# Reordering the split products of four down stages in an encoder trunk on one Trainium2 core

## The chip, the cores and the metric

The kernel runs on one core of one Trainium2 chip, in one launch. A core has five engines that work side by side, each on its own list of instructions: TensorE (PE in the profile, with PEld for its weight loads), VectorE (DVE), ScalarE (ACT), GpSimd (POOL) and SyncE (SP, which here only issues transfers). Sixteen DMA engines carry the transfers. The metric is the device time of one execution in microseconds; the time of a kernel is the median of its runs.

## The reference

A trunk of two layers over 512 positions of width 1024, in float32. Cut to what matters here:

```python
for i in range(DEPTH):                       # DEPTH = 2, D_MODEL = 1024, D_FF = 2816, SEQ = 512
    h = h + 0.5 * swiglu(rmsnorm(h, norm_ffn1[i]), ffn1_w_gate[i], ffn1_w_up[i], ffn1_w_down[i])
    hn = rmsnorm(h, norm_mix[i])
    h = h + (ab_mixer(hn, ...) if i % 2 == 0 else c_mixer(hn, ...))
    h = h + 0.5 * swiglu(rmsnorm(h, norm_ffn2[i]), ffn2_w_gate[i], ffn2_w_up[i], ffn2_w_down[i])
    gate = jax.nn.sigmoid(rmsnorm(h, norm_ple[i]) @ w_ple_gate[i])
    h = h + gate * (p[i] @ w_ple_proj[i])
return rmsnorm(h, norm_final)

def swiglu(x, w_gate, w_up, w_down):
    return (jax.nn.silu(x @ w_gate) * (x @ w_up)) @ w_down
```

The last product of `swiglu`, by `w_down` (2816 x 1024), is the down stage. There are four of them.

## The kernel before

Every float32 product is made of three matmuls: each operand is split into a rounded high part and the rest, and high x high, high x low and low x high are added up in PSUM. The split of a weight unit is `split` (lines 150 and 151): ScalarE copies the high part (`wh`), VectorE subtracts it from the raw weights to get the low part (`wl`). A raw unit is 128 x 1024 floats, 512 KB, and lies in a tile `wr`.

**Tiles.** Tiles of each kind come from a fixed number of slots: 5 `wr`, 4 each of `wh` and `wl`, 8 `tmp` of 128 x 512, 62 `act` of 128 x 512, and the PSUM banks 3 `mm`, 2 `sc`, 2 `tr` and 1 `ob`. A tile needs a slot before its first write, and waits until the last use of the tile that had the slot.

**Order.** A planner goes over the program once and fixes the order of the instructions on each engine by estimated times and priorities; the engines then execute in that order and wait for each other through semaphores. Within one kind of tile, slots are handed out in the order of the program. `high_priority()` moves instructions up, and `issue_after(x)` keeps the instructions issued inside it behind x on x's own engine.

**A down stage** (`down`, lines 434 to 620) has 22 chunks of 128 rows. The first four (`wide`, `xs`) are multiplied in the plain way by the `left` and `right` halves of the weights. The other 18 are taken as nine pairs (A, B), and w_down as four quarters b11, b12, b21 and b22 of nine chunks, and the block product is done with seven products in place of eight: some with sums of activations (`inner_sums`: x3), some with sums of weight quarters. Quarters come in five units: four of two chunks and one of one chunk. A weight sum is not calculated by an engine: `load` (L474, SP) brings one quarter to a `wr` tile, and `add` (L478, POOL) issues a second transfer that adds another quarter into the same tile, over and over along a chain:

```python
b11 -> r1 += x1,   + b12 -> r3 += x1 (right),    # group 1, r2 += x2 with b21 beside it
b12 + b22 -> rb += x3,  + b11 -> r1 += x3 (right),  + b21 -> rc += x2 (right)   # group 2
```

The order of a stage before is: rx (24 matmuls, the four wide chunks by `right`), copied to `cx`; group 1 in steps s = 0 to 5, where step s has r1 and r2 of unit s and the fifth product r3 of unit s-1; the left wide product into r2; the additions of r2 to the copies of r1 (L538); group 2 in steps s = 0 to 6, where step s has rb of unit s, r1 of unit s-1 and rc of unit s-2, and the left-hand wide product into rc in steps 0 and 1; and the tail: the right wide units once more, then b22 by x4, both into r3, among the transposes and the norm's splits. rc has the banks that r2 had, so its first product waits for L538. `halves` of 512 columns, as the pair stages of the feed-forward do them in tiles named `rb` (L366 to L369), are the only weight loads of 256 KB.

**The other places.** Each norm's sum of squares (`ssq`, L226) is turned into a factor per position by `stat`: eight small matmuls (L233), VectorE (L235), GpSimd's power (L236); `spread` transposes it (L252) and ScalarE copies it to `R` (L260). The property `rcol` makes the statistic on first use, and `R` the copy. In group c (the neighbourhood mixer, `c`, L1141) `self.rcol` stands first, and `project_v` (L694, matmuls L712 to L714) makes the values. The gate stage (`ple`, L1294) multiplies chunks 0 and 1 of the gate with the inner products first, then takes `R` and goes through the eight chunks, with t1 at L1333.

Of the kernel before, what the change touches and what calls it, by code (L numbers as in the profile page):

```python
# [10 lines left out]
F32R = mybir.dt.float32r  # L11
# [4 lines left out]
P = 128  # L16
# [32 lines left out]
class Trunk:  # L49
# [408 lines left out]
    def down(self, w, a, xs, sums, kept):  # L458
# [13 lines left out]
        def load(b, u):  # L472
            raw = self.wr.tile([P, UNIT], F32, tag="wr", name=self.nm("wr"))[:, :len(u) * T]
            nc.sync.dma_start(raw, b[:, u.start * T:u.stop * T])  # L474
            return raw

        def add(raw, b, u):
            nc.gpsimd.dma_start(raw, b[:, u.start * T:u.stop * T], accum_op=ALU.add)  # L478

        def product(out, u, ws, xs, cols, start=False, stop=False):  # L480
            mm = nc.tensor.matmul
            for j, k in enumerate(u):
                wh, wl = (x[:, j * T:(j + 1) * T] for x in ws)
                for i, p in enumerate(out):
                    c = slice(cols.start + i * P, cols.start + (i + 1) * P)
                    xh, xl = (x[:, c] for x in xs[k])
                    mm(p, xh, wh, start=start and k == 0, stop=False, skip_group_check=True)  # L487
                    mm(p, xh, wl, start=False, stop=False, skip_group_check=True)
                    mm(p, xl, wh, start=False, stop=stop and k == u.stop - 1, skip_group_check=True)

        def copied(p):
            out = [self.act() for _ in p]
# [4 lines left out]
        r1, r3 = [self.bank(), self.bank()], [self.sbank(), self.sbank()]  # L497
        r2 = [self.bank(), self.obank()]
        x1, x2, x3, x4 = ([None] * K2 for _ in range(4))
        n, raws = len(units), {}  # L500
        last = lambda u: u.stop == K2

        rx = [self.tbank(), self.tbank()]
        for u in wide:
            for k in u:
                xs[k] = xs[k] or self.split_chunk(a[k], nc.vector)
            product(rx, u, self.parts(load(right, u)), xs, r, True, u.stop == WHOLE)
        cx = copied(rx)

        def summed(s):  # L510
            raws[s] = load(b12, units[s])
            add(raws[s], b22, units[s])

        for s in range(n + 1):
            if s < n:
                u = units[s]
                raw = raws[s] = load(b11, u)
                for k in u:
                    if sums[k] is None:
                        sums[k] = self.inner_sums(A[k], B[k])  # L520
                    x1[k] = self.split_chunk(A[k], nc.vector)
                product(r1, u, self.parts(raw), x1, l, True, last(u))
                add(raw, b12, u)
                raw = load(b21, u)
                for k in u:
                    x2[k] = self.split_chunk(B[k], nc.vector)
                product(r2, u, self.parts(raw), x2, l, True)
            if s:
                u = units[s - 1]
                product(r3, u, self.parts(raws[s - 1]), x1, r, True, last(u))  # L530

        summed(0)
        ws = [self.parts(load(left, u)) for u in wide]
        for u, ww in zip(wide, ws):
            product(r2, u, ww, xs, l, False, u.stop == WHOLE)
        c11, c5 = copied(r1), cx
        for o, p in zip(c11, r2):
            tt(o, p, o, op=ALU.add)  # L538

        rb, rc = [self.tbank(), self.tbank()], [self.bank(), self.obank()]  # L540
        for s in range(n + 2):
            if s + 1 < n:
                summed(s + 1)
            if s < n:
                u = units[s]
                for k in u:
                    x3[k] = self.split_chunk(sums[k], nc.vector)
                    tt(B[k][:, l], B[k][:, l], sums[k][:, r], op=ALU.add)
                product(rb, u, self.parts(raws[s]), x3, l, True, last(u))
                add(raws[s], b11, u)  # L550
            if s < len(wide):
                product(rc, wide[s], ws[s], xs, r, True)
            if s == 1:
                for o, p in zip(c5, r3):
                    tt(o, p, o, op=ALU.add)
            if 0 < s <= n:
                u = units[s - 1]
                product(r1, u, self.parts(raws[s - 1]), x3, r, False, last(u))
                add(raws[s - 1], b21, u)
            if s == n + 1:  # L560
                c2 = copied(r1)
                u3 = [self.act(), self.act()]
                for i in range(2):
                    tt(u3[i], c2[i], rb[i], op=sub)
                for i in range(2):
                    tt(c5[i], c5[i], u3[i], op=sub)
            if s > 1:
                u = units[s - 2]
                product(rc, u, self.parts(raws[s - 2]), x2, r, False, last(u))
                for k in u:  # L570
                    t = self.act(F32R)
                    x4[k] = t[:, l], t[:, r]
                    self.split(B[k][:, l], *x4[k])
        c21 = [self.act(), self.act()]
        for i in range(2):
            tt(c21[i], rc[i], u3[i], op=ALU.add)
# [25 lines left out]
                self.h[m + j] = h  # L602
                self.norm_split(m + j, c)

        for u in wide:
            product(r3, u, self.parts(load(right, u)), xs, l)
        for i, u in enumerate(units):
            product(r3, u, self.parts(load(b22, u)), x4, l, False, last(u))
            if i < 2:
                second_half(M + 2 * i, c22, r)  # L610
            elif i < 4:
                first_half(2 * i - 4)
                first_half(2 * i - 3)
# [84 lines left out]
    def project_v(self, src, view, rcol, parts=True, banks=None):  # L698
# [5 lines left out]
        for q in range(2):  # L704
            u = self.unit(src[:, q * UNIT:(q + 1) * UNIT], lo_eng=self.lo_eng())
            for kk in range(4):
                k = 4 * q + kk
                h, l = (x[:, kk * 256:(kk + 1) * 256] for x in u)
                for b in range(NB):
                    xh, xl = (view(x, b) for x in self.xg[k])  # L710
                    first, last = k == 0 and b % 2 == 0, k == KC - 1 and b % 2 == 1
                    nc.tensor.matmul(ps[b], xh, h, start=first, stop=False, skip_group_check=True)  # L712
                    nc.tensor.matmul(ps[b], xh, l, start=False, stop=False, skip_group_check=True)
                    ins = nc.tensor.matmul(ps[b], xl, h, start=False, stop=last, skip_group_check=True)  # L714
            if q == 0:
                self.half_v = ins
        out = []
        for b in range(NB):
            r = rcol[:, b:b + 1]
# [111 lines left out]
    def ab(self, k_next):  # L831
# [60 lines left out]

        def proj_v(key, i):
            if i < 2:
                f = lambda: v.__setitem__(key, self.project_v(io["v_ab"][i], nat, self.rcol, banks=None if i else [
                    self.sbank(), self.bank()]))
            else:
                f = lambda: v.__setitem__(key, self.residues(
                    self.project_v(io["v_ab"][i], nat, self.rcol, parts=False)))
            return [(key, 2.4, f)]  # L900
# [239 lines left out]

    def c(self, k_next):  # L1141
        nc, io = self.nc, self.io
        self.rcol


        sel = [[self.act(F32R) for _ in range(2)] for _ in range(2)]
# [57 lines left out]

        first = [self.obank(), self.bank()]
        self.mm_units(first, [self.unit(io["qk_c"][i], lo_eng=self.lo_eng()) for i in range(2)])
        fill, steps = [], []
        for n in range(KC):
            fill += [(("q", n), 1, lambda n=n: proj_q(n, None if n else first[0])),
                     (("k", n), 1, lambda n=n: proj_k(n, None if n else first[1]))]  # L1210
            if n % 2 == 0:
                fill.append((("v", n // 2), 2, lambda i=n // 2: vs.__setitem__(
                    i, self.project_v(io["v_c"][i], nat, self.rcol, banks=None if i else [self.sbank(), self.bank()]))))
            need = [("q", n), ("k", n)]
            for hf in range(2):
                steps.append((need, 1, lambda n=n, hf=hf: soft(n, hf)))
                if (n, hf) == (KC - 1, 0):
                    begin = len(steps)
                if n + hf:
                    m, hm = (n, 0) if hf else (n - 1, 1)  # L1220
                    steps.append(([("v", m // 2)], 1, lambda m=m, hm=hm: pv(m, hm)))
# [73 lines left out]
    def ple(self, i, k_next, regroup):  # L1295
# [7 lines left out]
        up, ends, first = None, [], []  # L1303
        for m in range(KC):
            self.fetch(self.kept, m)
            u = first[m][0] if m < len(first) else self.unit(io["plg"][i, m])
            if m % 4 == 0:
                up = self.unit(io["plp"][i, m // 4])
            s = m % 4 * 2 * P
# [1 line left out]
            if m == 0:  # L1311
# [4 lines left out]
                        self.mm_unit(q, tuple(x[:, j * 2 * P:(j + 1) * 2 * P] for x in up), p, True, True)  # L1316

                self.mm_units([f[1] for f in first], [f[0] for f in first], inner)

            half = k_next == N_NORM - 1 and m == KC - 1  # L1320
            for x in (slice(0, T // 2), slice(T // 2, T)) if half else (slice(0, T),):
                cut = lambda parts: [tuple(y[:, x] for y in c) for c in parts]
                if m < len(first):
                    pg, pp = first[m][1:]
                else:
                    pg, pp = self.bank()[:, x], self.sbank()[:, x]
                    self.mm_unit(pg, u, cut(xg), True, True)
                    self.mm_unit(pp, upm, cut(p), True, True)
                if m == 0:
                    R = self.R  # L1330
# [205 lines left out]
```

## Time and profile before

| | |
|---|---|
| median of the runs | 2065.73 us (2065.39 to 2075.05, 3 runs) |
| the profiled execution | 2069.41 us, span 2067.6 us |
| granted TensorE clock, mean over it | 0.994 |
| TensorE busy | 2013.6 us in 12438 matmuls |
| VectorE, ScalarE, GpSimd busy | 1595.9, 1121.0 and 282.9 us |
| the four down stages | about 238 to 359, 880 to 1000, 1289 to 1408 and 1871 to 1992 us |

Busy time is the time in which an engine executed something; the span is from the first to the last instruction. A row "A <- B: total, times, longest" in the list of waits says that the instructions A stood idle until B was done. Timelines have start, duration, engine, line, operation and tiles, and in brackets the idle time before and its releaser. Windows give for each engine (TensorE, weight loads, VectorE, ScalarE, GpSimd) the busy time and the number of instructions in a stretch, then the granted clock, the DMA engines' busy share and GB/s.

### The profile page before, as it was taken

Reading aid. Unit: us, or ns where it says so; the run is one execution under the profiler, and the core shown is the slowest. Engines: PE = TensorE matmul, PEld = TensorE weight load, DVE = VectorE, ACT = ScalarE, POOL = GpSimd, SP = SyncE. Lnnn points to the kernel's source line nnn. Section 1 sums busy time; section 2 is a strip of 40 time slices with the busy share of each in tenths; the row PEclk is TensorE's granted clock in tenths of the full one; section 3 lists DMA queues with packets and bytes.
Section 4 is the critical chain, followed back from the end, with each engine's and each line's share of the span. In section 5 each row is a group of like instructions: output and inputs, shape, how many; then the busy total and the mean of one; then the engine's idle time right before and its main releaser. Section 6 shows DMA issues by size and latency. Waiting matters only on the chain.

```text
span 2067.6 us, 33144 instructions
## 1 busy us (share of the span) xinstructions
PE 2013.6 (97%) x12438; PEld 1786.7 (86%) x12438; DVE 1595.9 (77%) x2743; ACT 1121.0 (54%) x1898; POOL 282.9 (14%) x318
## 2 busy tenths in 40 slices
PE   9999999999999999999999999999999999999898
PEld 6999877879788899977789999778888889998776
DVE  8888866798766888876778888767788678888575
ACT  6455645477645455564544555645666445556452
POOL 0000021342212000012210000112000200001221
PEclk9999999999999999999999999999999999999999
DMA  6666679543425566579644666796333446666881
GB/s 195 179 183 180 166 175 259 168 93 81 98 62 173 128 179 184 161 176 214 229 153 128 184 174 175 183 221 196 108 112 98 160 116 174 179 164 169 187 275 41
DMA packets 126896, 334.90 MB, mean 162 GB/s; under 512 B 23696, under 2 KB 31376, under 8 KB 126736
## 3 DMA queue, kind: packets, MB, share of 16 engines
q1 hardware_dynamic: 98880, 245.71, 35.8%
q0 software_dynamic: 27712, 87.05, 24.1%
q8 instruction: 97, 1.59, 0.3%
q14 instruction: 63, 0.52, 0.1%
q10 hardware_dynamic: 144, 0.04, 0.0%
HBM read 304.42 MB, written 17.27 MB: 156 GB/s over the span
## 4 chain that ended last, share of the span: by engine, by line
PE 79%; DMA 7%; DVE 6%; issue 4%; ACT 3%; POOL 1%; SPq 0%; POOLq 0%; ACTq 0%; DVEq 0%
PE mm L391 6%; PE mm L390 6%; PE mm L392 6%; DMA wr<-in_dn_dram 5%; PE mm L176 5%; PE mm L175 5%; PE mm L177 5%; PE sc L392 3%; PE sc L391 3%; PE sc L390 3%; PE sc L175 2%; PE sc L177 2%; PE sc L176 2%; DVE wl L151 2%; PE ob L392 2%
## 5 line engine op out<-in xcount | busy, mean ns | idle before, releaser
L150 ACT ACTIVATE wh<-wr 128x1024 fp32r<-128x1024 f32 (+2 forms) x499 | 511.5, 1029 | 499.8 <-DMA wr<-in_dn_dram 126.5
L151 DVE TENSOR_TENSOR wl<-wr,wh 128x1024 fp32r<-128x1024 f32 (+2 forms) x499 | 594.2, 1195 | 190.5 <-ACT wh L150 186.2
L392 PE MATMUL mm<-act,wl 128*128 128x256 f32 x1088 | 307.9, 283 | 0.0
L391 PE MATMUL mm<-act,wh 128*128 128x256 f32 x1088 | 307.9, 283 | 0.0
L390 PE MATMUL mm<-act,wh 128*128 128x256 f32 x1088 | 307.9, 283 | 0.0
L175 PE MATMUL mm<-act,wh 128*128 128x512 f32 (+1 forms) x632 | 247.5, 393 | 1.1 <-ACT act L213 0.5
L177 PE MATMUL mm<-act,wl 128*128 128x512 f32 (+1 forms) x632 | 247.4, 391 | 0.5 <-DVE wl L151 0.5
L176 PE MATMUL mm<-act,wh 128*128 128x512 f32 (+1 forms) x632 | 247.1, 392 | 0.6 <-DVE act L214 0.6
L390 PEld LDWEIGHTS mm<-act,wh 128*128 128x128 f32 x1088 | 208.9, 192 | 0.2
L391 PEld LDWEIGHTS mm<-act,wh 128*128 128x128 f32 x1088 | 208.9, 192 | 0.2
L392 PEld LDWEIGHTS mm<-act,wl 128*128 128x128 f32 x1088 | 208.9, 192 | 0.0
L390 PE MATMUL sc<-act,wh 128*128 128x256 f32 x544 | 154.0, 283 | 0.0
L391 PE MATMUL sc<-act,wh 128*128 128x256 f32 x544 | 154.0, 283 | 0.0
L392 PE MATMUL sc<-act,wl 128*128 128x256 f32 x544 | 154.0, 283 | 0.0
L368 POOL DMA_DIRECT2D wr<-in_gu_dram x68 | 59.3, 872 | 678.0 <-DMA wr<-in_gu_dram 240.2
L176 PEld LDWEIGHTS mm<-act,wh 128*128 128x128 f32 x632 | 118.9, 188 | 23.9 <-DVE act L214 2.4
L175 PEld LDWEIGHTS mm<-act,wh 128*128 128x128 f32 x632 | 118.8, 188 | 23.7 <-ACT act L213 1.7
L177 PEld LDWEIGHTS mm<-act,wl 128*128 128x128 f32 x632 | 118.8, 188 | 22.3 <-DVE wl L151 1.3
L478 POOL DMA_DIRECT2D wr<-in_dn_dram x80 | 69.6, 944 | 420.5 <-DVE wl L151 319.6
L487 PE MATMUL mm<-wh,act 128*128 128x512 f32 x248 | 98.2, 396 | 13.8 <-DVE act L538 9.0
L151 DVE TENSOR_TENSOR act<-act,act 128x512 fp32r<-128x512 f32 (+1 forms) x176 | 105.9, 630 | 6.9 <-ACT act L150 6.9
L390 PEld LDWEIGHTS sc<-act,wh 128*128 128x128 f32 x544 | 104.4, 192 | 0.0
(253 smaller groups left out, 4746.1 us busy)
## 6 DMA issues: line engine op xcount, KB each, us to landing
wr<-in_gu_dram SPq DMA_DIRECT2D x176, 512.0 KB, 4.5
wr<-in_dn_dram SPq DMA_DIRECT2D x88, 512.0 KB, 4.3
wr<-in_gu_dram POOLq DMA_DIRECT2D x68, 512.0 KB, 5.5
wr<-in_dn_dram POOLq DMA_DIRECT2D x64, 512.0 KB, 6.3
rb<-in_gu_dram SPq DMA_DIRECT2D x68, 256.0 KB, 2.5
act<-kept SPq DMA_DIRECT2D x56, 256.0 KB, 5.6
wr<-in_qk_ab_dram SPq DMA_DIRECT2D x20, 512.0 KB, 4.0
kept<-act POOLq DMA_DIRECT2D x32, 256.0 KB, 3.0
```

The source lines that it names most:

```text
L150: self.put(self.nc.scalar.activation(hi, src, AF.Copy))
L151: self.put((lo_eng or self.nc.vector).tensor_tensor(lo, src, hi.bitcast(F32), op=ALU.subtract))
L175: mm(out, stat[0], mov[0], start=start, stop=False)
L176: mm(out, stat[0], mov[1], start=False, stop=False)
L177: return mm(out, stat[1], mov[0], start=False, stop=stop)
L368: nc.gpsimd.dma_start(rs, w[:, :UNIT], accum_op=ALU.add)
L390: mm(out, w[0][:, c], xs[k][0][:, x], start=start and k == 0, stop=False, skip_group_check=True)
L391: mm(out, w[0][:, c], xs[k][1][:, x], start=False, stop=False, skip_group_check=True)
L392: mm(out, w[1][:, c], xs[k][0][:, x], start=False, stop=stop and k == half - 1, skip_group_check=True)
L478: nc.gpsimd.dma_start(raw, b[:, u.start * T:u.stop * T], accum_op=ALU.add)
L487: mm(p, xh, wh, start=start and k == 0, stop=False, skip_group_check=True)
```

## The change

Five things are changed, and the matmuls remain the same in number.

1. In group 1 the fifth product r3 of unit s-2, not s-1, follows step s; the last two come behind the left wide product.
2. Group 2 begins with rb of unit 0 ahead of the left wide product; in its loop the order is seventh (rb), sixth (r1), fourth (rc). The wide rc product comes as a whole ahead of the loop, and the second use of the right wide units goes from the tail into steps 2 and 3. The differences u3 are taken one step earlier.
3. Weights that belong to no sum (right, left, b21 and b22) are loaded in halves of 256 KB to `tmp` tiles and split half by half (`halved`); `wr` is left to the chain of sums.
4. In c and ab the statistic of v's factor is issued behind the first half of the first v projection, which in c is traced ahead of the weave; `self.rcol` at the top of c goes.
5. In the gate stage chunk 2's 24 matmuls are issued ahead of the statistic, into a bank of their own.

```diff
+        def halved(b, u):
+            hi = self.wh.tile([P, UNIT], F32R, tag="wh", name=self.nm("wh"))
+            lo = self.wl.tile([P, UNIT], F32R, tag="wl", name=self.nm("wl"))
+            raws = [self.tmp() for _ in u]
+            for raw, k in zip(raws, u):
+                nc.sync.dma_start(raw, b[:, k * T:(k + 1) * T])
+            for j, raw in enumerate(raws):
+                c = slice(j * T, (j + 1) * T)
+                self.split(raw, hi[:, c], lo[:, c])
+            return hi, lo
...
-            product(rx, u, self.parts(load(right, u)), xs, r, True, u.stop == WHOLE)
+            product(rx, u, halved(right, u), xs, r, True, u.stop == WHOLE)
         cx = copied(rx)
+        rb = [self.tbank(), self.tbank()]
...
+        def first(s):
+            u = units[s]
+            raw = raws[s] = load(b11, u)
+            for k in u:
+                if sums[k] is None:
+                    with self.tc.issue_after(marks[s - 2].ins):
                         sums[k] = self.inner_sums(A[k], B[k])
+                x1[k] = self.split_chunk(A[k], nc.vector)
+            marks.append(product(r1, u, self.parts(raw), x1, l, True, last(u)))
+            add(raw, b12, u)
+        def second(s):                    # x2 splits, product(r2, u, halved(b21, u), x2, l, True)
+        def fifth(s):                     # product(r3, u, self.parts(raws[s]), x1, r, True, last(u))
+        def seventh(s):                   # x3 splits, product(rb, ...), add(raws[s], b11, u)
+        def sixth(s):                     # product(r1, ..., x3, r), add(raws[s], b21, u)
+        def fourth(s):                    # product(rc, ..., x2, r), x4 splits
...
+        for s in range(n):
+            first(s)
+            second(s)
+            if s > 1:
+                fifth(s - 2)
+        c11, c5 = copied(r1), cx
         summed(0)
-        ws = [self.parts(load(left, u)) for u in wide]
+        seventh(0)
+        ws = [halved(left, u) for u in wide]
         for u, ww in zip(wide, ws):
             product(r2, u, ww, xs, l, False, u.stop == WHOLE)
-        c11, c5 = copied(r1), cx
+        summed(1)
         for o, p in zip(c11, r2):
             tt(o, p, o, op=ALU.add)
+        fifth(n - 2)
+        fifth(n - 1)
+        rc = [self.bank(), self.obank()]
+        for u, ww in zip(wide, ws):
+            product(rc, u, ww, xs, r, True)
+        for o, p in zip(c5, r3):
+            tt(o, p, o, op=ALU.add)
+        for s in range(1, n + 2):
             if s + 1 < n:
                 summed(s + 1)
             if s < n:
+                seventh(s)
+            if s <= n:
+                sixth(s - 1)
+            if s > 1:
+                fourth(s - 2)
+            if s in (2, 3):
+                u = wide[s - 2]
+                product(r3, u, halved(right, u), xs, l)
+            if s == n:
                 c2 = copied(r1)
...
-        for u in wide:
-            product(r3, u, self.parts(load(right, u)), xs, l)
         for i, u in enumerate(units):
-            product(r3, u, self.parts(load(b22, u)), x4, l, False, last(u))
+            product(r3, u, halved(b22, u), x4, l, False, last(u))
... project_v
             if q == 0:
                 self.half_v = ins
+                if callable(rcol):
+                    with self.tc.issue_after(ins.ins):
+                        rcol = rcol()
... c
-        self.rcol
...
+        vs[0] = self.project_v(io["v_c"][0], nat, lambda: self.rcol, banks=[self.sbank(), self.bank()])
... ple
-            u = first[m][0] if m < len(first) else self.unit(io["plg"][i, m])
+            u = first[m][0] if m < len(first) else next_u if m == 2 else self.unit(io["plg"][i, m])
...
                 self.mm_units([f[1] for f in first], [f[0] for f in first], inner)
+                next_u, ahead = self.unit(io["plg"][i, 2]), self.bank()
+                self.mm_unit(ahead, next_u, xg, True, True)
...
-                    pg, pp = self.bank()[:, x], self.sbank()[:, x]
-                    self.mm_unit(pg, u, cut(xg), True, True)
+                    pg, pp = (ahead if m == 2 else self.bank())[:, x], self.sbank()[:, x]
+                    if m != 2:
+                        self.mm_unit(pg, u, cut(xg), True, True)
```

More of the change, by code (lines that the diff above doesn't have):

```diff
@@ L488, in product @@
                     mm(p, xh, wl, start=False, stop=False, skip_group_check=True)
-                    mm(p, xl, wh, start=False, stop=stop and k == u.stop - 1, skip_group_check=True)
+                    ins = mm(p, xl, wh, start=False, stop=stop and k == u.stop - 1, skip_group_check=True)
+            return ins
         def copied(p):
@@ L499, in down @@
         x1, x2, x3, x4 = ([None] * K2 for _ in range(4))
-        n, raws = len(units), {}
+        n, raws, marks = len(units), {}, []
         last = lambda u: u.stop == K2
@@ L512, in summed @@
             add(raws[s], b22, units[s])
[L514 to L519, printed above, removed]
-                        sums[k] = self.inner_sums(A[k], B[k])
[L521 to L530, printed above, removed]
+        def first(s):
[4 more added lines that the diff above has]
+                    with self.tc.issue_after(marks[s - 2].ins):
+                        sums[k] = self.inner_sums(A[k], B[k])
+                x1[k] = self.split_chunk(A[k], nc.vector)
+            marks.append(product(r1, u, self.parts(raw), x1, l, True, last(u)))
+            add(raw, b12, u)
@@ new lines, in second @@
+        def second(s):
+            u = units[s]
+            for k in u:
+                x2[k] = self.split_chunk(B[k], nc.vector)
+            product(r2, u, halved(b21, u), x2, l, True)
+        def fifth(s):
+            u = units[s]
+            product(r3, u, self.parts(raws[s]), x1, r, True, last(u))
+        def seventh(s):
+            u = units[s]
+            for k in u:
+                x3[k] = self.split_chunk(sums[k], nc.vector)
+                tt(B[k][:, l], B[k][:, l], sums[k][:, r], op=ALU.add)
+            product(rb, u, self.parts(raws[s]), x3, l, True, last(u))
+            add(raws[s], b11, u)
@@ new lines, in sixth @@
+        def sixth(s):
+            u = units[s]
+            product(r1, u, self.parts(raws[s]), x3, r, False, last(u))
+            add(raws[s], b21, u)
+        def fourth(s):
+            u = units[s]
+            product(rc, u, self.parts(raws[s]), x2, r, False, last(u))
+            for k in u:
+                t = self.act(F32R)
+                x4[k] = t[:, l], t[:, r]
+                self.split(B[k][:, l], *x4[k])
+        for s in range(n):
[3 more added lines that the diff above has]
+                fifth(s - 2)
@@ L532, in down @@
+        c11, c5 = copied(r1), cx
         summed(0)
-        ws = [self.parts(load(left, u)) for u in wide]
+        seventh(0)
+        ws = [halved(left, u) for u in wide]
         for u, ww in zip(wide, ws):
             product(r2, u, ww, xs, l, False, u.stop == WHOLE)
-        c11, c5 = copied(r1), cx
+        summed(1)
         for o, p in zip(c11, r2):
             tt(o, p, o, op=ALU.add)
-        rb, rc = [self.tbank(), self.tbank()], [self.bank(), self.obank()]
-        for s in range(n + 2):
+        fifth(n - 2)
@@ L544, in down @@
             if s < n:
[L545 to L560, printed above, removed]
+                seventh(s)
[7 more added lines that the diff above has]
+            if s == n:
                 c2 = copied(r1)
@@ L566, in down @@
                     tt(c5[i], c5[i], u3[i], op=sub)
[L567 to L573, printed above, removed]
         c21 = [self.act(), self.act()]
@@ L894, in proj_v @@
             if i < 2:
-                f = lambda: v.__setitem__(key, self.project_v(io["v_ab"][i], nat, self.rcol, banks=None if i else [
-                    self.sbank(), self.bank()]))
+                f = lambda: v.__setitem__(key, self.project_v(
+                    io["v_ab"][i], nat, self.rcol if i else lambda: self.rcol, banks=None if i else [self.sbank(), self.bank()]))
             else:
@@ L1210, in c @@
                      (("k", n), 1, lambda n=n: proj_k(n, None if n else first[1]))]
-            if n % 2 == 0:
+            if n % 2 == 0 and n:
                 fill.append((("v", n // 2), 2, lambda i=n // 2: vs.__setitem__(
-                    i, self.project_v(io["v_c"][i], nat, self.rcol, banks=None if i else [self.sbank(), self.bank()]))))
+                    i, self.project_v(io["v_c"][i], nat, self.rcol))))
             need = [("q", n), ("k", n)]
```

## The prediction

> **What bounds the kernel now.** I read the page first, then the waits of TensorE, then the timeline and the stage windows around the longest of them. Page, busy time:
>
> ```profile
> PE 2013.6 (97%) x12438; PEld 1786.7 (86%) x12438; DVE 1595.9 (77%) x2743; ACT 1121.0 (54%) x1898; POOL 282.9 (14%) x318
> ```
>
> TensorE is busy for 2013.6 of 2067.6 us, so the change, which leaves the number of matmuls as it is, can only shorten what TensorE waits for, and the time it loses at half clock. Its waits (releaser, then total us, times, longest):
>
> ```profile
> PE mm L487 <- DVE act L538: 9.0, 4, 3.9
> PE sc L488 <- DVE wl L151: 5.1, 6, 2.0
> PE mm L487 <- ACT act L150: 4.8, 4, 1.2
> PE tr L252 <- POOL rcol L236: 4.7, 4, 1.8
> PE tr L233 <- DVE ssq L226: 3.7, 2, 2.9
> PE ob L176 <- POOL act L151: 2.7, 4, 0.7
> PE sc L487 <- ACT wh L150: 2.6, 2, 1.8
> PE mm L488 <- DVE wl L151: 2.0, 6, 0.4
> ```
>
> L487 to L489 are the products of the four down stages. Rows one, two, seven and eight are 9.0 + 5.1 + 2.6 + 2.0 = 18.7 us in 18 waits, all in those stages. Row five is the norm sum ahead of the middle group c, row four mostly the gate products. Rows three and six are not touched.
>
> The longest wait of the third down stage, in the timeline of all engines (start, length, engine, line, idle before):
>
> ```profile
> 1341.54 1.06 ACT L150 ACTIVATE wh<-wr 128x1024 fp32r<-128x1024 f32 x1 [4.26 <-DMA wr<-in_dn_dram]
> ...
> 1342.49 0.39 PE L489 MATMUL tr<-wh,act 128*128 128x512 f32 x1
> ...
> 1342.63 1.23 DVE L151 TENSOR_TENSOR wl<-wr,wh 128x1024 fp32r<-128x1024 f32 x1 [3.06 <-ACT wh L150]
> ...
> 1346.17 0.68 DVE L538 TENSOR_TENSOR act<-ob,act 128x512 f32<-128x512 f32 x1
> 1346.31 0.19 PEld L487 LDWEIGHTS mm<-wh,act 128*128 128x128 f32 x1 [3.86 <-DVE act L538]
> 1346.31 0.50 PE L487 MATMUL mm<-wh,act 128*128 128x512 f32 x1 [3.44 <-DVE act L538]
> ```
>
> The reader is to see a chain that begins at a transfer: a summed weight lands, ScalarE splits it, VectorE stood idle 3.06 us for that split with the two additions of L538 queued behind, and the product rc, which wants the two banks that L538 reads, stands last. The late sum costs twice, at its own product and at the next one.
>
> **What one wait costs.** A run of 24 products in a row gives the cadence, from its first and its last:
>
> ```profile
> 1289.34 0.40 PE L487 MATMUL tr<-wh,act 128*128 128x512 f32 x1
> ...
> 1294.58 0.39 PE L489 MATMUL tr<-wh,act 128*128 128x512 f32 x1
> ```
>
> (1294.58 - 1289.34) / 23 = 0.228 us, so a unit of two chunks (12 matmuls) is 2.7 us and a step of three such units 8.2. From 1342.49 to 1346.31 are 3.82 us, 3.59 more than the cadence, where the row says 3.44; with a first matmul that is also slow to follow on I add 0.25 us to each wait. Then the clock (stretch, its length, five pairs of busy time, granted clock, DMA share, GB/s):
>
> ```profile
> 982.08:985.50 3.42, 3.42 (x10) 2.64 (x9) 1.97 (x2) 0.80 (x1) 0.00 (x0) 0.50 1.02 383
> ...
> 1930.98:1934.39 3.41, 3.41 (x10) 2.67 (x9) 2.50 (x6) 0.00 (x0) 0.00 (x0) 0.50 1.05 204
> 1425.81:1432.64 6.83, 6.45 (x30) 6.16 (x31) 1.58 (x5) 1.04 (x2) 1.03 (x1) 0.50 0.00 0
> ```
>
> These are the first and the last of three such stretches in down stages, and the one in c. At 0.50 half of 3.41 us is lost, 1.7 us. What comes before the first of them is this:
>
> ```profile
> 980.70 0.50 PE L488 MATMUL sc<-wl,act 128*128 128x512 f32 x1 [1.82 <-DVE wl L151]
> ```
>
> A wait of 1.82 us, next to some shorter ones, was followed by half clock. [...]
>
> **The change, part by part.**
>
> Down, gross. 18.7 us of waits, 18 x 0.25 = 4.5 for restarts, 3 x 1.7 = 5.1 of clock: 28.3 us in four stages. What removes them:
>
> (1) Two steps between a sum and its use. The sum is issued by POOL on a tile that has just been split. How long it takes to land:
>
> ```profile
> DMA to landing us min/median/max: 4.4/6.5/11.3
> ```
>
> (the answer for L478). With the full-width splits
>
> ```profile
> L150 ACT ACTIVATE wh<-wr 128x1024 fp32r<-128x1024 f32 x466 | 491.8, 1058 | 445.3 <-DMA wr<-in_dn_dram 85.4 <-PE mm L176 70.4 <-ACT wh L150 52.7
> ```
>
> that chain is 6.5 + 1.06 + about 1.2 on VectorE = 8.8 us at the median and 13.6 at the most. Before, the last fifth product has two units of cover, 5.4 us: it waits. After, at least seventh(0), two wide left units and a second's product lie between, 11 us or more: the median is covered, the maximum nearly. (2) rc now follows fifth(n-2) and fifth(n-1), 4.1 us behind the last read of its banks where it was one unit, 2.7; and L538 no longer queues behind a split that waits for a transfer, since seventh(0) is ahead of it. (3) The right wide units leave the tail for steps 2 and 3, and no longer wait there. (4) `issue_after(marks[s-2].ins)` names a TensorE instruction around three VectorE ones; as an order within an engine it holds nothing back, zero. I keep 2.3 us of small waits: down is -26.
>
> Down, new work. Some 15 units a stage are now loaded and split in halves. Rows of existing halves and wholes, transfer (KB, median us to landing) and split:
>
> ```profile
> wr<-in_gu_dram SPq DMA_DIRECT2D x176, 512.0 KB, 4.5
> ...
> rb<-in_gu_dram SPq DMA_DIRECT2D x68, 256.0 KB, 2.5
> ...
> wr<-in_dn_dram SPq DMA_DIRECT2D x16, 256.0 KB, 4.6
> ```
> ```profile
> L150 ACT ACTIVATE wh<-rb 128x512 fp32r<-128x512 f32 x68 | 42.4, 623 | 0.0
> ```
>
> Two halves on ScalarE are 1.25 us for 1.06, 15 x 0.19 = 3 us a stage; VectorE's part grows alike, and SP has 15 more issues. What hides them is the idle share of each:
>
> ```profile
> 1285.00:1346.00 61.00, 56.28 (x260) 45.36 (x258) 46.88 (x69) 37.60 (x57) 10.47 (x12) 1.00 0.75 182
> 1346.00:1408.00 62.00, 61.69 (x277) 51.06 (x278) 41.27 (x58) 29.96 (x42) 8.11 (x11) 0.97 0.92 239
> ```
>
> VectorE (third pair) is busy 46.9 and 41.3 us, ScalarE 37.6 and 30.0, so zero on average; but the 5.5 us of wide products that covered VectorE in the tail are gone, and I charge 0.25 us a stage, 1 us in all, with bounds 0 and 8 (2 us a stage, the longest wait on a split, row two).
>
> (5) rx starts later. Its four halves now need `tmp` tiles, and slots go out in the order of the program, so theirs come behind those of the last pair of ffn, whose last one is used here:
>
> ```profile
> 1288.32 0.69 DVE L413 TENSOR_TENSOR tmp<-sc,tmp 128x512 f32<-128x512 f32 x1
> ```
>
> rx began at 1289.34 with no wait, as its `wr` tiles were loaded before. If the load goes out only with L413: 1288.32 + 2.5 to land (4.6 by the slower row) + 0.62 + 0.7 of splits = 1292.1 (1294.2), a wait of 2.8 (4.9) us. If SP runs ahead: 0. L413's row does not show whether SP is held by it, so I take the middle of 0 and 2.8, rounded up to 1.5 us: 4 x 1.5 = +6 us, bounds 0 and 4 x (4.9 + 1.7) = 26.
>
> (6) Group c. L233 is put behind 48 of v0's matmuls; only 24 stood ahead of it:
>
> ```profile
> 1422.56 0.28 PE L714 MATMUL mm<-wh,act 128*128 128x256 f32 x1
> 1425.71 1.74 PE L233 MATMUL tr<-ones,ssq 128*128 128x1 f32 x8 [2.87 <-DVE ssq L226]
> ...
> 1428.89 1.12 PE L252 MATMUL tr<-ident,rcol 128*128 128x128 f32 x4 [0.38 <-POOL rcol L236]
> ```
>
> At 0.12 us each (half the width of the others) the other 24 fill 2.9 of the 2.87 + 0.25. The 6.83 us at half clock go with it, half of that, but little more than 3 us, as waiting for L252 is part of it. With 0.38 + 0.25 that is 6.7 at best; if L252 then waits for ScalarE and POOL with nothing left of v0, up to 3 us come back. I take -5.5, bounds -6.7 and -2. In ab the same edit meets no wait of L233 in the list beyond row five: zero.
>
> (7) Gate products (twice). 24 matmuls of chunk 2 now go ahead of the norm sum:
>
> ```profile
> 1017.80 0.95 PE L233 MATMUL tr<-ones,ssq 128*128 128x1 f32 x8
> ```
> ```profile
> 1021.09 0.65 PE L252 MATMUL tr<-ident,rcol 128*128 128x128 f32 x4 [1.76 <-POOL rcol L236]
> ...
> 1027.49 0.39 PE L175 MATMUL mm<-act,wh 128*128 128x512 f32 x1
> ```
> ```profile
> 1022.41 0.69 DVE L1333 TENSOR_TENSOR tmp<-mm,R 128x512 f32<-128x512 f32 x1 [2.27 <-ACT R L260]
> ```
>
> That the planner puts L233 where the program has it, next to the end of the opening products, moves it 24 x 0.228 = 5.5 us later. Then only 6 matmuls (1.4 us) are left to cover the 3.29 us from L233 to L252, and chunk 3 has to wait for the bank that L1333 frees, some 1.9 us behind L252 (1022.41 + 0.6 - 1021.09): 1017.80 + 5.5 + 3.29 + 1.9 = 1028.5, where chunk 3 began at 1027.49 before. +0.65 to +1 each, +1.3 in all; if L233 keeps its place, 2 x (1.76 + 0.2) = -3.9.
>
> Sum: -26 + 1 + 6 - 5.5 + 1.3 = -23 us. The profiled execution took 2069.41 us (span 2067.6), so 2046 against itself; the runs shown have a median of 2065.73, and from that, 2043.
>
> **The rivals.**
>
> (A) All of it hides: no wait at rx, all 28.3 of down, 6.7 in c, 3.9 at the gates: -39, 2027. For it: SP is not held by tiles that are free. Against it: (5) and (7).
>
> (B) rx is late by the bound: +26 for +6, so -3, 2063. For it: the 4.6 us row, and a half clock after 1.82 us of waiting.
>
> (C) Halves make the transfers the bound. Two of 2.5 us for one of 4.5 is 0.5 us more for a unit, 15 x 0.5 = 7.5 us a stage, +30 in all: 2073. It decides only where the engines have no room for it; the two stretches above leave 0.25 x 61 + 0.08 x 62 = 20 us a stage, but the second of them little. If a third of it shows, 2053. [...]
>
> (D) Slower: a halved load queues on SP behind a whole load that waits for its slot, as whole loads do for the sums now:
>
> ```profile
> SPq L474 <- DMA wr<-in_dn_dram: 158.8, 24, 24.2
> ```
>
> 158.8 / 24 = 6.6 us on average. Once a stage, at rx or b21, with a half clock it is 4 x (6.6 + 1.7) = 33 in place of 6: +4, 2070; it decides from (23 + 6) / 4 = 7.3 us a stage, and twice a stage gives 2103.
>
> (E) Two steps are not enough, as the sums land late in the full second half: half of the 26 stays, -10, 2056.
>
> **How the numbers follow.** Chances: forecast 0.52 (2034 to 2052), A 0.16, B 0.09, C 0.08, D 0.06, E 0.09. The time is the forecast's, 2043. Leaving out the top of B and C, all of D and the end of A gives 2027 to 2058 for 8 in 10. Half a per cent is 10.3 us, about what a measurement of this kernel tells from no change: below 2055.4 are the forecast, A, a good half of C and half of E, 0.79; above 2076 only D's second form and bad mixtures, 0.05; the rest is 0.16.
>
> **What would show it.** Right: the row of L487 behind L538 gone or under 2 us, the two rows of sc at L487 and L488 under 2 us together, L233 in c under 0.5, no half clock in the down stages; a new row of tr at L487 waiting for a split, 4 to 8 us in 4 times; at the gates L252 still waiting, or the chunk 3 product on VectorE's L1333. Wrong: rx waits above 5 us a stage (B, D), SP waiting at the halved load for `wl`, DMA share at 1 through the first half of the stage (C), or rows of `wl` in the loop of sums (E).

## The result, and the profile after

| | before | changed |
|---|---|---|
| median | 2068.70 us (2065.39 to 2075.41, 8 runs) | 2051.72 us (2049.37 to 2059.09, 8 runs) |
| ratio | | 0.992, 95% interval 0.990 to 0.994 |
| profiled span | 2067.6 us | 2048.4 us |

The changed kernel is faster by 0.8% (0.6 to 1.0), some 17 us; its profiled execution is 19.2 us shorter than that of before. The busy line of the page after:

```profile
PE 2008.8 (98%) x12438; PEld 1786.9 (87%) x12438; DVE 1598.8 (78%) x2799; ACT 1127.6 (55%) x1954; POOL 280.3 (14%) x318
```

The number of matmuls is the same, so the 19 us are waits and clock. TensorE's waits after, the longest rows (releaser, then total us, times, longest):

```profile
PE tr L498 <- ACT wh L150: 8.5, 4, 2.1
PE mm L498 <- ACT act L150: 4.8, 4, 1.2
PE tr L252 <- POOL rcol L236: 4.3, 3, 1.8
PE tr L1410 <- ACT tmp L1404: 1.7, 1, 1.7
PE ob L176 <- POOL act L151: 1.4, 2, 0.7
PE tr L233 <- DVE ssq L226: 1.4, 2, 0.8
```

(L498 to L500 are now the products of the down stage, L489 the sum.) The reader is to see that the four rows of before in the down stages, 18.7 us in 18 waits, are gone (4.4 us of them, the wait of 1.82 us at 980.70 among them, stood in the tail at the right wide units, whose weights are no sum); that L233 in c waits 0.66 us (the shorter one of its two) where it waited 2.9; that the old wait at the first r1 product stands as it was; and that the first row is new: rx waits for a split, 2.1 us in each of the four stages.

For a ledger I took, between each two successive starts of matmuls in a trace, the time above the usual cadence of that shape, and summed it by stage. That has the waits, the slow restarts and the half clock in it. It comes from one trace of each kernel, and a stretch at half clock more or less (1.7 us) is in it by chance:

| above the cadence, us | before | changed |
|---|---|---|
| four down stages, rx to the last transpose | 38.7 | 24.6 |
| group c up to the first attention step | 7.35 | 1.71 |
| two gate stages, opening to chunk 3 | 9.8 | 12.3 |
| all else, difference | | -2 |

-14.1 - 5.6 + 2.5 - 2 = -19, the difference of the spans.

What the new wait consists of, in the third down stage of the changed kernel (SP, ScalarE, VectorE and TensorE from the timelines):

```profile
1278.25 9.82 SPq L482 DMA_DIRECT2D tmp<-in_dn_dram  x11
```
```profile
1283.35 0.38 ACT L414 ACTIVATE act<-mm 128x256 f32<-128x256 f32 x1 [2.49 <-PE mm L392]
1284.22 0.63 ACT L416 ACTIVATE act<-act 128x512 f32<-128x512 f32 x1 [0.49 <-DVE act L415]
1284.76 1.66 ACT L150 ACTIVATE wh<-tmp 128x512 fp32r<-128x512 f32 x3
```
```profile
1281.91 0.69 DVE L413 TENSOR_TENSOR tmp<-sc,tmp 128x512 f32<-128x512 f32 x1 [0.60 <-PE sc L392]
```
```profile
1285.42 0.73 PE L498 MATMUL tr<-wh,act 128*128 128x512 f32 x2 [2.11 <-ACT wh L150]
```

SP began to issue the halves at 1278.25, 3.7 us ahead of L413, and the first two had landed at 1281.8 and 1282.5. ScalarE then stood idle until 1283.35, for 2.49 us, in front of L414, and took the first half of rx only behind L414 and L416. So the data was there, and the place in ScalarE's order was not. The planner had put the splits there; that it does so because rx's `tmp` slots are handed out after the last pair's is what the first two experiments are to show. Three of these four waits are followed by half clock (granted clock in the column behind the five pairs; the third stage is the one without):

```profile
240.00:243.40 3.40, 3.03 (x7) 2.34 (x8) 3.40 (x6) 3.40 (x7) 0.00 (x0) 0.53 0.55 180
877.70:882.00 4.30, 4.18 (x10) 3.06 (x11) 4.30 (x8) 3.54 (x6) 0.53 (x1) 0.60 0.65 198
1285.40:1288.80 3.40, 3.30 (x13) 2.46 (x14) 3.40 (x7) 3.40 (x6) 0.00 (x0) 1.00 0.61 191
1858.00:1861.40 3.40, 3.40 (x8) 2.71 (x9) 3.40 (x6) 2.67 (x5) 0.50 (x1) 0.52 0.84 238
```

### The profile page after: what moved, and what is told of

Its sections match the earlier page's. It is cut to its first block, busy times and chain, and to the rows that moved or that the text cites. A ratio compares the mean times of both kernels' runs of the same rounds, so it can differ in the third digit from the quotient of the medians.

```text
span 2048.4 us, 33392 instructions
## 1 busy us (share of the span) xinstructions
PE 2008.8 (98%) x12438; PEld 1786.9 (87%) x12438; DVE 1598.8 (78%) x2799; ACT 1127.6 (55%) x1954; POOL 280.3 (14%) x318
## 4 chain that ended last, share of the span: by engine, by line
PE 73%; DVE 3%; issue 2%; ACT 2%; POOL 0%; DVEq 0%; ACTq 0%; POOLq 0%
PE mm L176 5%; PE mm L175 5%; PE mm L177 5%; PE mm L392 5%; PE mm L391 5%; PE mm L390 5%; PE sc L391 2%; PE sc L390 2%; PE sc L392 2%; PE mm L498 2%; PE mm L500 2%; PE mm L499 2%; PE sc L177 2%; PE sc L175 2%; PE sc L176 2%
## 5 line engine op out<-in xcount | busy, mean ns | idle before, releaser
L150 ACT ACTIVATE wh<-wr 128x1024 fp32r<-128x1024 f32 (+2 forms) x435 | 448.1, 1032 | 431.1 <-PE mm L176 61.2
L151 DVE TENSOR_TENSOR wl<-wr,wh 128x1024 fp32r<-128x1024 f32 (+2 forms) x435 | 524.0, 1206 | 153.4 <-ACT wh L150 151.7
L489 POOL DMA_DIRECT2D wr<-in_dn_dram x80 | 69.3, 879 | 427.8 <-DVE wl L151 220.0
L150 ACT ACTIVATE act<-act 128x512 fp32r<-128x512 f32 (+1 forms) x176 | 96.9, 577 | 19.5 <-PE sc L500 8.5
```

The costliest lines, as they stand in the source:

```text
L150: self.put(self.nc.scalar.activation(hi, src, AF.Copy))
L151: self.put((lo_eng or self.nc.vector).tensor_tensor(lo, src, hi.bitcast(F32), op=ALU.subtract))
```

## The experiments

Theory 1 is that rx waits for its place in ScalarE's order, set by the `tmp` slots; theory 2 that its weights land late. Beside it stands the question which part of the change did away with the waits on weights inside the stage. Each ratio is against the kernel before.

**rx whole again.**

```diff
-            product(rx, u, halved(right, u), xs, r, True, u.stop == WHOLE)
+            product(rx, u, self.parts(load(right, u)), xs, r, True, u.stop == WHOLE)
```

> The changed kernel, but rx's two units are loaded whole into wr tiles again. Theory 1 (order of the tmp slots): the halves of rx land in time, and it is their splits that stand behind the last pair's work on ScalarE, because their slots come after that pair's in the program; with wr the wait at rx (8.5 us in 4, and three half-clock stretches of 1.5 us each behind it) goes, some 13.5 us, to about 0.985 of before, 0.993 of the changed kernel. Theory 2 (transfer): rx's weights land late because the DMA engines are busy; then whole loads land no earlier, the wait stays at 2 us a stage and the time is that of the changed kernel. A third way: two wr tiles for rx hold up the first loads of b11, and a wait of 2 us or more turns up at the first r1 product, half of the gain.

Measured: 2038.37 us (2036.82 to 2042.33), ratio 0.9858 (0.9844 to 0.9872): 13 us less than the changed kernel. Row one of the waits is gone; the list now begins so:

```profile
PE mm L498 <- ACT act L150: 6.5, 4, 2.4
PE tr L252 <- POOL rcol L236: 4.3, 3, 1.8
```

The down stages have 11.2 us above the cadence for 24.6. Part of the third way shows too: the first r1 product waits 1.7 us longer in all.

**rx in halves, but in a wr tile** (two loads of 256 KB into the halves of one `wr` tile, split half by half).

> The changed kernel, with rx's units still loaded and split in halves of 256 KB, but into the two halves of a wr tile. Theory 1: as with whole loads, the wait at rx goes, 0.985 of before. If it is the halves themselves (more issues on SP, four splits in place of two), the wait stays at about 2 us a stage and the ratio at 0.992.

Measured: 2038.09 us (2035.72 to 2041.26), ratio 0.9852 (0.9835 to 0.9868), as with whole loads. With this run the halves themselves are out as the cause: same loads, same splits, another kind of tile, and no wait. The kind of tile moves two things, though: the splits stand ahead of the last L414 on ScalarE, and the loads too go out earlier, the second unit's 21 us ahead of rx. That ScalarE's order and not the landing made the wait is seen in the changed kernel itself, where the first halves had landed while ScalarE was idle. Theory 1 holds and theory 2 falls.

**The order alone** (all loads whole; the changed c and gate stages stay).

```diff
+        halved = lambda b, u: self.parts(load(b, u))
```

> The changed kernel with all loads whole in wr tiles, so the new order of products alone. If the order is what removed the waits on sums, none of 3 us comes back, rx has no wait either, and the ratio is 0.985 or a little above. If the tiles set free by the halves were needed, sums are issued late for want of a wr slot: waits on wl or wh at L498 to L500 of 10 us or more in all over four stages, and the ratio is 0.992 or worse.

Measured: 2061.78 us (2057.93 to 2065.69), ratio 0.9971 (0.9960 to 0.9981). 34.6 us above the cadence in the down stages, against 38.7 before. TensorE waits at two new places, the first seventh product and, in the tail, the second unit of b22:

```profile
PE tr L489 <- ACT act L150: 7.3, 4, 2.1
PE sc L490 <- DVE wl L151: 5.9, 4, 1.6
```

The first of them is a late sum, although the row names a split of activations: that split stands on ScalarE behind the one of a summed weight, for which ScalarE waits, here in the first stage:

```profile
278.28 1.06 ACT L150 ACTIVATE wh<-wr 128x1024 fp32r<-128x1024 f32 x1 [6.56 <-DMA wr<-in_dn_dram]
```

So the order by itself wins 4 us in the down stages.

**The halves alone**, in the old order and with the old c and gate stages (`right`, `left`, b21 and b22 by `halved`).

> The kernel before with halves in tmp tiles for right, left, b21 and b22, its order of products kept. If the order did the work, all waits of before stay (18.7 us in the four rows) and the wait at rx is added, 8 to 14 us: ratio 1.004 to 1.007. If the free wr slots did part of it, L538 and the splits of sums wait less by that part, and the ratio is 1.000 or below.

Measured: 2059.20 us (2057.73 to 2063.59), ratio 0.9960 (0.9946 to 0.9973), although rx's wait is in it, as the first row of TensorE's waits shows:

```profile
PE tr L498 <- ACT wh L150: 8.4, 4, 2.1
```

None of the four rows of before is left. A sum of group 1 begins with a load of b11 and one of group 2 with a load of b12, and when SP issues it tells why. These are b12's loads of unit 0 in the third stage, before and with the halves alone (SP's whole loads counted in the order of the program):

```profile
1316.64 0.33 SPq L474 DMA_DIRECT2D wr<-in_dn_dram  x1
```
```profile
1299.12 0.33 SPq L474 DMA_DIRECT2D wr<-in_dn_dram  x1
```

| issue of a load, us after rx's first product, third stage | before | order alone | halves alone | changed |
|---|---|---|---|---|
| b11, last unit (group 1) | 20.9 | 25.3 | -9.4 | -9.4 |
| b12, unit 0 | 27.3 | 27.3 | 14.4 | 18.2 |
| b12, unit 1 | 37.3 | 43.7 | 22.5 | 27.0 |

What SP waits for in front of b12's loads is the split that frees a `wr` slot. So sums were late because the load that begins one had to wait for a slot, which the unsummed units used as well; the order alone lets it go no earlier. The total of SP's waits would mislead here. The row at L474 behind transfers is 158.8 us before and almost gone with the halves alone:

```profile
SPq L474 <- DMA wr<-in_dn_dram: 3.8, 4, 2.4
SPq L167 <- DMA wr<-in_dn_dram: 122.9, 19, 19.9
```

But of the 158.8 us only the first wait of each stage, 21 us in all, stands in front of a load of b12. The rest holds up loads of the tail, and with the halves the wait for the same slots is at L167, in front of the next stage's weights, and no new row of TensorE's waits comes of it.

The statement that two steps do away with the waits is wrong as it stands. One thing is left open: no run loads the unsummed weights whole into slots of their own, so a part of the smaller transfers and splits in the gain is not excluded. At rx, where the halves were tried in a `wr` tile, they made no difference.

**Halves with rx whole, old order, old c and gate.**

> The kernel before with halves in tmp tiles for left, b21, b22 and the second use of right, rx whole in wr, and its order of products, its group c and its gate stage kept. Theory: the late sums were a matter of wr slots, not of steps; then the four rows of sums stay away, rx has no wait, what is left against the changed kernel with rx whole (2038) is c's 5.6 us and some 3 to 5 us of small waits in the stages: about 2046, ratio 0.989. Rival: the order in two steps is needed once rx takes two wr tiles again; then L538's successor waits 2 us or more in some stages and the ratio is 0.993 or worse.

Measured: 2045.35 us (2044.64 to 2046.51), ratio 0.9894 (0.9879 to 0.9909). 12.8 us above the cadence in the down stages, where the new order has 11.2 (rx whole): in this setting the order is worth 1.6 us, which is no more than one stretch at half clock.

**c undone** (on rx whole).

> The changed kernel with rx whole, and group c as in the kernel before. The ledger of the two traces gives 5.6 us to c's change: L233's wait of 2.9 us and the 6.8 us at half clock behind it come back, 2044, ratio 0.988. If that half clock depends only on where the gap falls in time, L233's 2.9 us come back without it: 2041.

Measured: 2044.43 us (2041.36 to 2049.13), ratio 0.9891 (0.9872 to 0.9910): c's change is worth 6 us by the medians, 5.6 by the ledger.

**The gate stage undone** (on rx whole).

> The changed kernel with rx whole, and the gate stage as in the kernel before. Theory: the chunk put ahead hides nothing, as L233 went behind it: L252's waits of 1.76 us are there either way; its cost in the trace is the half clock behind that wait (1.5 us, twice), less 0.8 us at ob. Then this is 0 to 3 us faster than 2038, ratio 0.984 to 0.9855. Rival: the chunk ahead hides something that the ledger misses, and this is slower by 2 us or more.

Measured: 2035.83 us (2034.88 to 2041.41), ratio 0.9857 (0.9836 to 0.9877): 2.5 us less by the medians and nothing by the ratios. The chunk put ahead hides nothing.

**R taken ahead of chunk 2.**

```diff
+                self.R
                 next_u, ahead = self.unit(io["plg"][i, 2]), self.bank()
```

> The changed kernel with rx whole, and in the gate stage R is taken ahead of chunk 2's 24 matmuls in the program, so that they can cover the way from L233 to L252. Theory: the wait at L252 (1.76 us, twice) goes, and the half clock behind it: 4 to 7 us, 2031 to 2034, ratio 0.982 to 0.984. Rival: ssq is not ready so early, L233 waits for it by as much, and the ratio stays at 0.9855.

Measured: 2034.86 us (2033.55 to 2035.12), ratio 0.9842 (0.9827 to 0.9856). 3.5 us less than with rx whole alone, with intervals that overlap, and only by one of two waits being shorter: the timeline of TensorE in the first layer shows two matmuls between L233 and L252 and the rest of the chunk behind.

```profile
1003.39 0.95 PE L233 MATMUL tr<-ones,ssq 128*128 128x1 f32 x8
1004.20 0.48 PE L177 MATMUL mm<-act,wl 128*128 128x512 f32 x1
1004.52 0.40 PE L175 MATMUL mm<-act,wh 128*128 128x512 f32 x1
1005.71 0.65 PE L252 MATMUL tr<-ident,rcol 128*128 128x128 f32 x4 [0.80 <-POOL rcol L236]
```

ssq was ready, so the rival falls; but the planner puts L252 too early. That it counts on a shorter power on GpSimd (L236) than the 1.96 us that this took at the median in the changed kernel would explain it, and was not shown.

**R held behind chunk 2.**

```diff
+                self.rcol
                 next_u, ahead = self.unit(io["plg"][i, 2]), self.bank()
                 self.mm_unit(ahead, next_u, xg, True, True)
+                with self.tc.issue_after(self.last_mm.ins):
+                    self.R
```

> The changed kernel with rx whole, and in the gate stage the statistic (L233) ahead of chunk 2's 24 matmuls and R's transposes (L252) held behind the last of them. Theory: what decides is how much work lies between L233 and L252, and the planner by itself puts two matmuls there; with 24 the wait of 1.76 us goes in both layers and no half clock follows: 4 to 7 us less than 2038, 2031 to 2034, ratio 0.982 to 0.984. Rival: the first gate product's bank then comes free later, and chunk 3 waits for L1333 by as much: 2036 to 2038.

Measured: 2032.52 us (2030.11 to 2034.26), ratio 0.9826 (0.9812 to 0.9839), 5.9 us less than with rx whole alone. L252 no longer waits at the gates. What is late next is the bank of chunk 3, the second mechanism of step (7), with its price:

```profile
PE mm L175 <- DVE tmp L1375: 2.0, 2, 1.0
```

**The copies cx later** (on the kernel before this).

```diff
-        cx = copied(rx)
-        rb = [self.tbank(), self.tbank()]
...
             first(s)
+            if s == 0:
+                cx = copied(rx)
+                rb = [self.tbank(), self.tbank()]
```

> As the kernel before this, and in the down stage the copies cx of rx are issued behind the first product r1 in the program. Theory: the wait at the first r1 product (1.2 to 2.4 us in each stage) comes from x1's slots, which are handed out behind cx's, so that x1's split stands behind the copies on ScalarE; with the copies later it goes, 5 to 7 us: 2026 to 2029, ratio 0.979 to 0.981. Rival: rb or r1 then waits for the `tr` banks or ScalarE by as much, and nothing is won.

Measured: 2026.77 us (2026.28 to 2030.16), ratio 0.9802 (0.9789 to 0.9816): the fastest of all, 25 us below the changed kernel. 3.7 us above the cadence are left in four down stages. Its page:

```profile
PE 2001.0 (99%) x12438; PEld 1782.8 (88%) x12438; DVE 1597.2 (79%) x2791; ACT 1126.6 (56%) x1946; POOL 281.3 (14%) x318
```

**The same with the old order of products.**

> The same as the last kernel in all but the order of the products in the down stage, which is that of the kernel before (with the halves, rx whole and cx later). Theory: the order itself is worth little once the wr slots are free, 1 to 4 us: ratio 0.980 to 0.983. Rival: with the other waits gone the order in two steps carries 6 us or more, ratio 0.984 or above.

Measured: 2042.14 us (2040.60 to 2042.79), ratio 0.9872 (0.9858 to 0.9885). Here the rival is right: 15 us. The waits that are new with it are the r1 and r2 products of unit 1, for splits of activations, and the transposes of the tail:

```profile
PE mm L500 <- DVE act L151: 4.1, 8, 0.6
PE tr L596 <- DVE act L627: 4.0, 4, 1.1
...
PE tr L596 <- DVE act L612: 1.9, 2, 1.7
```

The later copies cost the old order 7 us (20.0 above the cadence in the down stages for 12.8) and gain the new one 8 (3.7 for 11.6; 5.8 by the medians). So by these single traces what the order is worth depends on what else is in place: 4 us without the halves, 1.6 with them, 16 with cx later as well. Why the later copies disturb the old order was not taken further.

## Why the prediction was right or wrong

**The time.** 2043 was forecast and 2051.7 measured, in the range of 2027 to 2058, on the side that was forecast; the forecast gain of 23 us was 17 by the medians and 19 by the profiles. Of the signs that were named, the rows of L538 and of the splits went, rx got its row (8.5 us, a little above the 4 to 8) and L252 still waits at the gates; but L233 in c has 0.66 us and not under 0.5, and three stretches at half clock are left in the down stages, all at rx.

**(1) to (3), sums.** Gross, the waits on weights inside the stage were put at -26 and the new work at +1. With rx's part (below) taken out of the -14.1 of the ledger, about -27.7 is left. The size is right and the cause is wrong, so that the size agrees is luck: the mechanism it was worked out from, units of cover between a sum and its use, won 4 us by itself. The step that failed is (1): it started its chain from the summing transfer, and the load that the sum begins with was late because SP had no slot for it (27.3 us after rx's first product before, 14.4 with the halves alone). Rival D read the row of 158.8 us at L474 as loads for the sums; only some 21 us of it are that. The charge of 0.25 us for a restart was too high as well: 3.59 less 3.44 is 0.15, and rx's waits of 2.11 us cost 2.27, 0.16 more. The summing transfers themselves did not get faster: they took 6.5 us to land at the median before, 5.8 with the order alone, where waits on them remain, and in the changed kernel, where none does:

```profile
DMA to landing us min/median/max: 4.0/7.1/10.5
```

With the halves alone the waits were gone. The new work, charged 1 us, shows in no row of waits.

**(5), rx.** This is the term that was mis-sized: +6 forecast, 9.1 us in waits and about 4.5 in three half-clock stretches measured, 13.6; without it 2038.4, by the first two experiments. That rx would wait was right, and the cause half right: the slots, yes, but by way of ScalarE's order, not of the transfer. The estimate started from L413 with a landing; the halves were under way before it (over the whole stage they took 5.1 us to land at the median, but rx did not wait for that). What sets the end is L416's turn on ScalarE, and I had left the rows of L414 and L416 out. The stretch at half clock stood in the upper bound alone.

**(6), c.** -5.5 forecast, -5.6 in the ledger and 6 by experiment. As feared, L233 still waits, 0.66 us in the timeline; but L252 does not, as the second half of v0 stands between them, and the clock in that stretch is full:

```profile
1416.81 1.02 PE L233 MATMUL tr<-ones,ssq 128*128 128x1 f32 x8 [0.66 <-DVE ssq L226]
...
1423.54 0.60 PE L252 MATMUL tr<-ident,rcol 128*128 128x128 f32 x4
```

**(7), gates.** +1.3 forecast, +2.5 in the ledger. L233 did go behind chunk 2, as expected. L252 however waits the old 1.76 us, as only two matmuls were put between; chunk 3 does not wait for its bank, and what is lost is clock:

```profile
1014.93 0.95 PE L233 MATMUL tr<-ones,ssq 128*128 128x1 f32 x8
...
1016.05 0.40 PE L176 MATMUL sc<-act,wh 128*128 128x512 f32 x1
1018.21 0.94 PE L252 MATMUL tr<-ident,rcol 128*128 128x128 f32 x4 [1.76 <-POOL rcol L236]
```
```profile
1018.40:1021.80 3.40, 3.40 (x11) 2.59 (x11) 0.69 (x1) 2.51 (x3) 0.00 (x0) 0.51 0.39 147
```

**The rivals.** A's gain, all of it hidden, is what the fastest kernel has with three further edits (-41 us). B is the direction that came true, at 13.6 of its 26 us. C does not show: the DMA share is 0.55 to 0.84 in the rows of rx and 0.87 over the first half of the third stage (0.75 before), not 1, and rx in halves costs nothing in a `wr` tile (2038.09 us, 2038.37 with whole loads): at rx what counted was whose tile a load occupies, not its size. D's sign is there and its price is not: SP does wait at halved loads for a split, but no wait of TensorE in the down stages comes of it.

```profile
SPq L482 <- DVE wl L151: 97.4, 74, 4.5
```

E does not show in the changed kernel.

## What to carry to other kernels

Where a transfer is late, look first at when it could be issued: a wait of the queue that issues loads, on a slot, can look like a wait of the matrix engine on a split, and giving other loads another kind of tile removed all four such rows here (18.7 us in 18 waits). Take the moment of issue of the very load in question for this, not the total of the queue's waits, most of which may belong to loads that nothing is waiting for. Where tiles are handed out in the order of the program, a kind of tile also carries an order with it: a load moved to a kind that the stage before it uses can get its place behind that stage on the engine that splits it, as rx did on ScalarE (2.1 us of waiting in each stage), even where the data has landed. And to cover a chain, count the instructions that the schedule puts between its first and its last, not those that are free to stand there.

## What the runs showed of the hardware

Half clock came, among others, after waits of 1.8 and of 2.1 us, and not each time. The wait of 1.76 us at L252 in the gate stage was followed by a stretch at 0.50 in both layers of the changed kernel, where it ends at 1018.21 and 1997.65 us. With rx in halves in a `wr` tile it ends at 1014.80 and 1987.52 us, and the next matmuls start 0.43 us apart, where 0.23 is usual. In the kernel before, the clock is 1.00 behind both (1021.09 and 2013.90 us). Of the four waits of 2.1 us at rx in the changed kernel three are followed by half clock; with the halves alone, those of the third and the fourth stage are. Apart from the one at the very end of each trace, the stretches in the kernel before and in the changed one are 3.41 or 6.83 us long; in the changed kernel there are five, all of 3.41 us, three at rx (from 240.20, 878.49 and 1858.11 us) and two at the gates (1018.44 and 1998.06).

So a wait of 2.1 us at rx cost 2.27 us where the clock stayed full and some 3.8 where half clock followed ((13.6 - 2.27) / 3). What decides between the two was not shown. The times of the changed kernel differ by up to 10 us from run to run (2049.37 to 2059.09); the mean granted clock was 0.995 in its fastest run and 0.992 in its slowest. How much of the 10 us comes from this was not tested.
